# A hybrid encoder layer on one core: rounded bias product, joined value products, and the recurrent row factor behind the projection

## The chip, the core and the metric

The kernel runs on one core of a Trainium2 chip. A core has a matrix engine (TensorE, PE in the profile, with its weight loads as PEld), a vector engine (VectorE, DVE), an activation engine (ScalarE, ACT), GpSimd (POOL), a queue engine (SyncE, SP) and 16 DMA engines that all queues share. The metric is the device time of one execution in microseconds; for several runs the median is given.

## The reference, cut to what matters

One encoder layer for a sequence of 512 positions and a width of 1024, in float32:

```python
h = rms_norm(x, attn_norm_g)
xr, gate, q, k, v = split(h @ w_in)
xr = centred_depthwise_conv(xr, conv_w, conv_b)
y_rnn = (rg_lru(xr, fwd) + rg_lru(xr, bwd)) * gelu(gate)
y_attn = dilated_attention(q, k, v, rel_bias)      # 8 heads of 64, three dilated windows
mix = concat([rms_norm(y_rnn, norm_rnn_g), rms_norm(y_attn, norm_attn_g)])
x = x + mix @ w_out
x = x + square(relu(rms_norm(x, mlp_norm_g) @ w_up)) @ w_down
return rms_norm(x, final_norm_g)
```

The three windows of the attention are computed as one: a key counts as often as windows hold it, and the logarithm of that count, or -1e30 for a key in none, joins the relative bias in one table over the distance. That table is the "bias table" of this document. An RMSNorm divides each position by the root of its mean square; that factor is one number per position, a "row factor", and may be applied behind a matrix product that mixes features only.

## The kernel before, in words

Activations lie with features on the 128 partitions and the 512 positions along the free axis, so a projection of 128 output features is a chain of products of 128 x 128 by 128 x 512. Each float32 operand is split into a rounded high part (dtype fp32r) and a residue; `mm3` makes three rounded products of them (high x high, high x low, low x high). ScalarE makes the high parts (`conv_hi`, L192, tile whi) and VectorE the residues (`conv_lo`, L199, tile wlo) of every weight block. Blocks come through SyncE's queue into three buffers wraw; the next one is asked for when `conv_lo` has read the last. Products of plain float32 operands are used for transposes (`pt`, `prow`), for column sums (`pcs`), for the bias table and for the value products.

The order on every engine is written out by hand. The stages that matter here:

1. The input projection's first three blocks (pxr), the column sums of squares and the first row factor (`rstd_cols`, `row_tile`). The recurrent gate weights come on SyncE's queue (gwr, L231). On ScalarE's queue come relt (33 x 8: the bias of each of 32 buckets for 8 heads, and a row of ones) and oht (two halves of 33 x 512: one-hot rows for the distances, and the row with the logarithm).
2. A loop of 32 steps n for the value projection (pv). Between its steps stand the recurrent gates (`lru_gate`, pg, evacuated by ScalarE into ga), `lru_x` (VectorE, L407) and, at n == 18, `bias_prep`: two products of relt and oht (L348), negated by VectorE (nbs, L350), written to DRAM (nbd) and read back per head as overlapping rows (tw).
3. The gate projections, then q and k for pair 0 of heads.
4. A loop over five rounds i of four steps u. Step (i, u) makes the scores of pair i for query tile u (`att_s`, `att_e`), the transposes of pair i-1's exponentials (`att_t`) and some of its value products (`att_av`). Into this loop a list of fillers puts q and k of the next pairs and, behind them, `wo_thunks(0, c2)`: the output projection of the recurrent half. A dictionary `plan` keyed (i, u, slot) holds the rest: squares (`sq_`), their sum (`add`), column sums (`rnn_cols`), the row factor (`rnn_rows`), the multiplication by it (`scaled`), and the splits (`hi`, `lo`).
5. The output projection of the attention half, then the feed-forward block, which takes more than half of the time and is not touched.

Tiles of 128 x 512 share a pool of 48 buffers (tag "g"); the PSUM banks are four of tag "pj" (projections, value products, bias), two of "gs" and two of "et".

The value products of a pair are eight: four key tiles times two heads of 64 columns each, which write the two halves of one PSUM tile. They are issued in two calls:

```python
            if u == 2 and i >= 1:
                att_av(i - 1, (0, 1))
...
            if u == 0 and i >= 2:
                att_av(i - 2, (2, 3))
```

Of the kernel before, what the change touches and what calls it, by code (L numbers as in the profile page):

```python
# [12 lines left out]
FT = mybir.dt.float32  # L13
FR = mybir.dt.float32r
AF = mybir.ActivationFunctionType
OP = mybir.AluOpType

P = 128
S = 512
D = 1024  # L20
KD = D // P
NH = 8
DH = 64
NBUCK = 32
# [16 lines left out]
for _n, _w in (("ag", 8), ("w0", 4), ("w1", 4), ("w2", 4), ("w3", 4), ("cb", 4),  # L41
# [2 lines left out]
    VEC[_n] = _o  # L44
    _o += _w
NVEC = _o


def bias_onehot():
    rel = np.arange(-(S - 1), S)  # L50
    m = np.zeros(rel.shape, np.int64)
    for window, dil in PATTERNS:
        half = window // (2 * dil)
        m += (rel % dil == 0) & (np.abs(rel) <= half * dil)
    nb = NBUCK // 2
    me = nb // 2
    n = np.abs(rel)
    nf = np.maximum(n, 1).astype(np.float32)
    large = me + (np.log(nf / np.float32(me)) / np.float32(math.log(MAXD / me))
                  * np.float32(nb - me)).astype(np.int32)  # L60
    large = np.minimum(large, nb - 1)
    bucket = np.where(rel > 0, nb, 0) + np.where(n < me, n, large)
    oh = np.zeros((NBUCK + 1, 2 * S), np.float32)
    oh[NBUCK, :] = NEG
    idx = np.arange(rel.size)
    keep = m > 0
    oh[bucket[keep], idx[keep]] = 1.0
    oh[NBUCK, idx[keep]] = np.log(m[keep].astype(np.float64)).astype(np.float32)
    return oh


@with_exitstack
def hybrid_kernel(ctx: ExitStack, tc, xw, xT, w_in, w_v, w_out, w_up, w_dn, gates, vecs, rel, onehot, fg, out):
    nc = tc.nc
    consts = ctx.enter_context(tc.tile_pool(name="consts", bufs=1))
    big = ctx.enter_context(tc.tile_pool(name="big", bufs=1))
    stream = ctx.enter_context(tc.tile_pool(name="stream", bufs=3))
    work = ctx.enter_context(tc.tile_pool(name="work", bufs=1))
# [6 lines left out]
    NG = 48  # L85

    def g_(name, dt=FT, shape=(P, S)):
        return work.tile(list(shape), dt, name=name, tag="g", bufs=NG)
# [7 lines left out]
    def f(t):  # L96
        return t.bitcast(FT)
# [237 lines left out]
            mm3(pxr[t], wk(t, k), hk(k), False, k == KD - 1)  # L335


    relt = consts.tile([NBUCK + 1, NH], FT, name="relt")
    nc.scalar.dma_start(relt, rel)
    oht = [work.tile([NBUCK + 1, S], FT, name="oht", tag="g", bufs=NG) for _ in range(2)]  # L340
    for i in range(2):
        nc.scalar.dma_start(oht[i], onehot[:, i * S:(i + 1) * S])
    nbd = dram.tile([NH, 2 * S], FT, name="nbd")

    def bias_prep():
        for i in range(2):
            pbz = ps_("pbias", "pj")
            nc.tensor.matmul(pbz[0:NH, :], lhsT=relt, rhs=oht[i], start=True, stop=True)  # L348
            nbs = g_("nbs", shape=(NH, S))
            nc.vector.tensor_scalar(nbs, pbz[0:NH, :], -1.0, None, op0=OP.mult)  # L350
            nc.scalar.dma_start(nbd[:, i * S:(i + 1) * S], nbs)
# [135 lines left out]
    def y_hi(k, y):  # L487
        ycat[k] = (g_("yh", FR), g_("yl", FR))
        act(ycat[k][0], y, AF.Copy, scale=vec("yg", k))

    def y_lo(k, y):
        hi, lo = ycat[k]
        stt(lo, y, vec("yg", k), f(hi), op0=OP.mult, op1=OP.subtract)

    yrnn = {}
    rr = {}
# [6 lines left out]
    def rnn_rows():  # L503
        rr[0] = row_tile(rc[0], "et")

    def rnn_scaled(*ts):
        for t in ts:
            nc.vector.tensor_tensor(yrnn[t], yrnn[t], rr[0], op=OP.mult)

    def rnn_split(*ts):  # L510
        for t in ts:
            y_hi(t, yrnn[t])
        for t in ts:
            y_lo(t, yrnn.pop(t))

    def proj_thunks(c, tag, done):
        o = {}

# [58 lines left out]
    def lru_hooks(n):  # L577
        m = n - GA
        if m in (11, 12, 14, 15):
            lru_x({11: 0, 12: 1, 14: 2, 15: 3}[m])  # L580
        if m in (12, 13, 20, 22):
            lru_exp({12: 0, 13: 1, 20: 2, 22: 3}[m])
        if m in (16, 17, 27, 28):
            t = {16: 0, 17: 1, 27: 2, 28: 3}[m]
            lru_sqrt(t)
            scans.extend(scan_ops(t)[:4])
        if n in SC:
            scans.popleft()()
# [4 lines left out]
    for n, (k, tt) in enumerate(steps):  # L593
        c = C_V + k // 2
        if k == 0:
            pv[tt] = ps_("pv", vtag[tt])
        hi, lo = splits[c]
        sl = slice((k % 2) * S, (k % 2 + 1) * S)
        tsl = slice(tt * P, (tt + 1) * P)
        mm3(pv[tt], (h_hi[:, k, tsl], h_lo[:, k, tsl]), (hi[:, sl], lo[:, sl]), k == 0, k == KD - 1)  # L600
        if n >= 16:
            feed(c, n % 8)
        if n in (8, 11, 14):
            conv_hi({8: 6, 11: 7, 14: 8}[n])
        if n in (9, 12, 15):
            conv_lo({9: 6, 12: 7, 15: 8}[n])
        if n >= GA and n < GA + 12 and (n - GA) % 3:
            t, m = (n - GA) // 3, 2 * ((n - GA) % 3 - 1)
            lru_gate(t, m)
            lru_gate(t, m + 1)  # L610
        if n == 0:
            conv_lo(5)
            conv_b(2)
        if n == 2:
            conv_b(3)
        if n == GA + 1:
            conv_h(2)
            conv_c(2)
        if n == GA + 2:
            conv_h(3)  # L620
            conv_c(3)
        lru_hooks(n)
        if n == 18:
            bias_prep()
            load_tw(0)
            load_tw(1)
    vs = big.tile([P, 4, S], FT, name="vs", tag="bigC")
    last = [scan_ops_end(t) for t in range(4)]
# [115 lines left out]
    def att_av(p, jts):  # L744
        if 0 in jts:
            pav[p] = ps_("pav", "pj")
        for jt in jts:
            for e in range(2):
                a = slice(64 * e, 64 * e + 64)
                h = 2 * p + e  # L750
                nc.tensor.matmul(pav[p][a, :], lhsT=vs[:, jt, h * DH:(h + 1) * DH], rhs=et.pop((h, jt)),  # L751
                                 start=jt == 0, stop=jt == 3)
        if 3 in jts:
            y = g_("yp")
            nc.vector.tensor_tensor(y[:, ::-1], pav.pop(p), zrow.pop(p), op=OP.mult)
            y_sq(y, 1)
            y_hi(4 + p, y)
            y_rest[p] = y
# [16 lines left out]
    x1 = {}  # L775
# [6 lines left out]
    def wo_thunks(half, c2):  # L782
        c = C_WO + half * 4 + c2
        o = {}

        def mk(j, k):
            def run():
                if k == 0:
                    o["p"] = ps_("pwo", "pj")
                mm3(o["p"], wok(c, j, k), ycat[half * 4 + k], k == 0, k == 3)  # L790
                feed_q(c, 4 * j + k)
                if k == 3:
                    cc = 2 * c2 + j
                    nc.vector.tensor_tensor(x1[cc], x1[cc], o["p"], op=OP.add)
            return run
        return [mk(j, k) for j in range(2) for k in range(4)]

# [31 lines left out]
    def rnn_sq(t):  # L829
        y_sq(yrnn[t], 0)  # L830

    def scaled(t):
        return lambda: rnn_scaled(t)

    def hi(t):
        return lambda: y_hi(t, yrnn[t])

    def lo(t):
        return lambda: y_lo(t, yrnn.pop(t))

    def end(t):
        return lambda: rnn_end(t)

    def sq_(t):
        return lambda: rnn_sq(t)

    def add():
# [3 lines left out]
    plan = {(0, 0, 2): [sq_(0), add], (0, 0, 3): [end(1)],  # L851
            (0, 1, 1): [sq_(1)],
            (0, 2, 3): [add],
            (1, 0, 2): [end(2)], (1, 0, 4): [sq_(2)],
            (1, 1, 0): [add], (1, 1, 2): [end(3)], (1, 1, 4): [sq_(3)],
            (1, 2, 0): [add], (1, 2, 2): [rnn_cols], (1, 3, 1): [rnn_rows],
            (1, 3, 3): [scaled(0)], (1, 3, 4): [scaled(1), hi(0), hi(1)],
            (2, 1, 2): [lo(0), lo(1)], (2, 1, 3): [scaled(2), scaled(3), hi(2), hi(3)], (2, 2, 2): [lo(2), lo(3)]}
    for i in range(3):
        for key, (is_k, fn, e) in {(0, 2): (1, s_hi, 0), (0, 3): (1, s_hi, 1), (1, 0): (1, s_lo, 0), (1, 1): (1, s_lo, 1),  # L860
                                   (2, 2): (0, s_hi, 0), (2, 3): (0, s_hi, 1), (3, 0): (0, s_lo, 0), (3, 1): (0, s_lo, 1)}.items():
# [13 lines left out]
    for i in range(5):  # L875
        for u in range(4):
            if i < 4:
                att_s(i, u)
                if u == 0 and i < 3:
                    load_tw(2 * i + 2)  # L880
                if u == 2 and i < 3:
                    load_tw(2 * i + 3)
            if i >= 1:
                att_t(2 * i - 2, u)
                att_t(2 * i - 1, u)
            if i < 4:
                att_e(i, u)
            if u == 2 and i >= 1:
                att_av(i - 1, (0, 1))
            if u == 0 and i >= 1:  # L890
                att_z(i - 1)
            if u == 0 and i >= 2:
                att_av(i - 2, (2, 3))
            beside(i, u, 0)
            fill(1)
            beside(i, u, 1)
            fill(1)
            if u == 1 and i >= 1:
                att_r(i - 1)
            if u == 0 and i >= 2:  # L900
                att_y(i - 2)
            beside(i, u, 2)
            fill(1)
            beside(i, u, 3)
            fill(1)
            beside(i, u, 4)
# [25 lines left out]
    wo_b(0, 0)  # L932
    wo_b(0, 1)
    conv_hi(c + 3)
    att_av(3, (2, 3))
    att_y(3)
    wo_b(0, 2)
    for k in range(3):
# [160 lines left out]
    ts = None  # L1099
    nr2 = {}  # L1100
    for half in range(2):
# [4 lines left out]
        start = 0  # L1106
        if half == 0:
            start = 3
# [13 lines left out]
        for ff in range(start, HF):  # L1122
            p = ps_("pu", "pj")
# [12 lines left out]
            if ff == 11 - 8 * half:  # L1136
                if half == 0:
                    ts = big.tile([P, NQ, 1024], FT, name="ts", tag="bigA")
# [57 lines left out]
        for j in range(7 * NQ):  # L1196
            _, w, q = seq[j]
# [94 lines left out]
```

## Time and profile before

| | |
|---|---|
| median of 3 runs | 569.79 us (569.21 to 570.31) |
| profiled execution | 569.28 us |
| its span, first to last instruction | 567.5 us |
| TensorE busy | 555.4 us (98%) |
| VectorE busy | 388.8 us (69%) |
| ScalarE busy | 313.7 us (55%) |
| moved by DMA | 82.97 MB, 146 GB/s over the span |
| mean granted TensorE clock | 0.996 |

Times in rows of the profile are microseconds from the start of the span unless marked ns. A row of a timeline gives start, length, engine, line, operation, "out<-in", partitions x elements and count, and in brackets how long the engine was idle before it and what ended that. Matmuls are pipelined: one starts before the last has ended, so the distance of two starts tells what one costs. A float32 matmul appears as two records. In rows of waits the columns are the total, the number of waits and the longest.

### The profile page before, as it was taken

The numbers are of one execution on the slowest core, as the hardware profiler recorded it, in microseconds if no ns is written. First come the engines' busy times: TensorE is split into PE (matmuls) and PEld (weight loads), VectorE is DVE, ScalarE is ACT, GpSimd is POOL, SyncE is SP. The second block draws the span as 40 slices with busy tenths as digits, with TensorE's granted clock in tenths as the row PEclk, the third lists the DMA queues.
The fourth block names the chain that finished last, engine by engine and source line by source line (L and its number), as shares of the span: only waits on it lengthen the run. The fifth ranks groups of instructions, "written<-read, shape, count | busy, mean of one in ns | idle before, by whom it ended". The sixth has DMA issues, their size and how long they took to land.

```text
span 567.5 us, 6886 instructions
## 1 busy us (share of the span) xinstructions
PE 555.4 (98%) x2520; PEld 444.8 (78%) x2520; DVE 388.8 (69%) x610; ACT 313.7 (55%) x510; POOL 50.1 (9%) x70
## 2 busy tenths in 40 slices
PE   9999999999999999999999999999999999999993
PEld 7877788677777768888888888888888888888782
DVE  6696499986865429553468778978243676896894
ACT  7659993687865525245354466653223243665654
POOL 3450000000000000000002133001000000131000
PEclk9999999999999999999999999999999999999998
DMA  7623424453261112242239799959623234699603
GB/s 261 233 74 113 147 102 142 110 160 121 75 223 38 51 59 77 76 148 75 79 111 288 173 268 273 262 174 254 196 74 112 74 112 94 196 252 262 161 1 148
DMA packets 25494, 82.97 MB, mean 146 GB/s; under 512 B 3106, under 2 KB 3234, under 8 KB 25460
## 3 DMA queue, kind: packets, MB, share of 16 engines
q1 hardware_dynamic: 19968, 64.50, 33.1%
q0 software_dynamic: 4608, 16.78, 15.5%
q10 hardware_dynamic: 884, 1.25, 0.6%
q8 instruction: 20, 0.33, 0.2%
q14 instruction: 14, 0.11, 0.1%
HBM read 78.81 MB, written 2.13 MB: 143 GB/s over the span
## 4 chain that ended last, share of the span: by engine, by line
PE 80%; DVE 10%; DMA 4%; ACT 3%; issue 2%; SPq 0%; ACTq 0%; DVEq 0%
PE pu L223 10%; PE pu L224 10%; PE pu L225 10%; PE pd L224 6%; PE pd L223 6%; PE pd L225 6%; PE pqk L223 3%; PE pwo L223 3%; DVE wlo L199 3%; PE pav L751 3%; PE pqk L225 3%; PE pwo L225 3%; PE pwo L224 3%; PE pqk L224 3%; PE pt L718 2%; DMA wraw<-in_w_dn_dram 2%
## 5 line engine op out<-in xcount | busy, mean ns | idle before, releaser
L199 DVE TENSOR_TENSOR wlo<-wraw,whi 128x1024 fp32r<-128x1024 f32 x81 | 99.9, 1234 | 38.4 <-ACT whi L192 38.3
L192 ACT ACTIVATE whi<-wraw 128x1024 fp32r<-128x1024 f32 x81 | 85.5, 1055 | 40.0 <-PE pd L225 17.7
L223 PE MATMUL pu<-h2h,whi 128*128 128x512 f32 x256 | 100.4, 392 | 0.0
L225 PE MATMUL pu<-h2h,wlo 128*128 128x512 f32 x256 | 99.7, 390 | 0.0
L224 PE MATMUL pu<-h2l,whi 128*128 128x512 f32 x256 | 99.6, 389 | 0.0
L224 PE MATMUL pd<-wlo,ah 128*128 128x512 f32 x192 | 74.8, 390 | 0.4 <-DVE wlo L199 0.4
L223 PE MATMUL pd<-whi,ah 128*128 128x512 f32 x192 | 74.7, 389 | 0.0
L225 PE MATMUL pd<-whi,al 128*128 128x512 f32 x192 | 74.7, 389 | 0.0
L1015 ACT ACTIVATE a<-pu 128x512 f32<-128x512 f32 x32 | 19.0, 598 | 97.9 <-PE pu L225 97.9
L1016 DVE TENSOR_TENSOR a<-a 128x512 f32<-128x512 f32 x32 | 22.0, 691 | 65.8 <-ACT a L1015 65.8
L225 PEld LDWEIGHTS pu<-h2h,wlo 128*128 128x128 f32 x256 | 48.0, 188 | 10.1
L223 PEld LDWEIGHTS pu<-h2h,whi 128*128 128x128 f32 x256 | 48.1, 188 | 9.8
L224 PEld LDWEIGHTS pu<-h2l,whi 128*128 128x128 f32 x256 | 48.1, 188 | 9.7
L224 PEld LDWEIGHTS pd<-wlo,ah 128*128 128x128 f32 x192 | 36.0, 188 | 8.1 <-DVE wlo L199 0.8
L223 PEld LDWEIGHTS pd<-whi,ah 128*128 128x128 f32 x192 | 36.0, 188 | 7.5
L225 PEld LDWEIGHTS pd<-whi,al 128*128 128x128 f32 x192 | 36.0, 188 | 7.5
L192 ACT ACTIVATE whi<-ts 128x1024 fp32r<-128x1024 f32 x24 | 25.5, 1060 | 23.7 <-PE pd L225 17.7
L199 DVE TENSOR_TENSOR wlo<-ts,whi 128x1024 fp32r<-128x1024 f32 x24 | 29.3, 1221 | 8.4 <-ACT whi L192 8.0
L223 PE MATMUL pqk<-h_hi,whi 128*128 128x512 f32 x64 | 26.5, 414 | 0.0
L205 POOL DMA_DIRECT2D ts<-in_w_dn_dram x16 | 16.9, 1203 | 106.7 <-DVE wlo L199 106.7
L223 PE MATMUL pwo<-yh,whi 128*128 128x512 f32 x64 | 26.3, 412 | 0.0
L720 ACT ACTIVATE ett<-pt 128x512 f32<-128x512 f32 x32 | 17.3, 591 | 15.7 <-PE pt L718 15.7
(210 smaller groups left out, 1029.5 us busy)
## 6 DMA issues: line engine op xcount, KB each, us to landing
wraw<-in_w_up_dram SPq DMA_DIRECT2D x32, 512.0 KB, 3.3
wraw<-in_w_dn_dram SPq DMA_DIRECT2D x24, 512.0 KB, 6.7
ts<-in_w_dn_dram POOLq DMA_DIRECT2D x24, 512.0 KB, 12.1
wraw<-in_w_in_dram SPq DMA_DIRECT2D x13, 512.0 KB, 3.3
wraw<-in_w_out_dram SPq DMA_DIRECT2D x8, 512.0 KB, 3.3
ts<-in_w_dn_dram SPq DMA_DIRECT2D x8, 512.0 KB, 4.9
tw<-in_w_dn_dram SPq DMA_DIRECT2D x8, 512.0 KB, 6.2
tw<-in_w_dn_dram POOLq DMA_DIRECT2D x8, 512.0 KB, 11.4
```

The source lines that it names most:

```text
L192: act(hi, raws[i], AF.Copy)
L199: nc.vector.tensor_tensor(lo, r, f(splits[i][0]), op=OP.subtract)
L205: nc.gpsimd.dma_start(r, wblock(c[0], nxt[1], c[2]), accum_op=OP.add)
L223: nc.tensor.matmul(o, lhsT=a[0], rhs=b[0], start=bool(first), stop=False)
L224: nc.tensor.matmul(o, lhsT=a[0], rhs=b[1], start=False, stop=False)
L225: nc.tensor.matmul(o, lhsT=a[1], rhs=b[0], start=False, stop=bool(last))
L718: nc.tensor.transpose(pt[:, qt * P:(qt + 1) * P], en[h][qt][:, jt * P:(jt + 1) * P], ident)
L720: act(t, pt, AF.Copy)
L751: nc.tensor.matmul(pav[p][a, :], lhsT=vs[:, jt, h * DH:(h + 1) * DH], rhs=et.pop((h, jt)), start=jt == 0, stop=jt == 3)
L1015: act(r, p, AF.Relu)
L1016: nc.vector.tensor_tensor(r, r, r, op=OP.mult)
```

## The change

Three edits.

The first concerns the bias table. The three inputs of the table are laid out on 97 rows: the 32 buckets, the 32 buckets again, the last row, 31 rows of zeros, and the last row again; relt is also padded to 128 columns. `bias_round` makes rounded copies of both, in which the second copy of the bias holds the residue of the rounding, and the last row of oht holds the residue of the logarithm's row. One rounded product then sums high and low parts. `bias_round` runs on VectorE at steps n = 14 (relt and the first half) and n = 16 (the second half).

The second puts all eight value products of a pair into one call, where the second call stood.

The third no longer multiplies y_rnn by its row factor before the output projection. The splits are made from the unscaled values, and each of the eight output sums is multiplied by the row factor when it is read from PSUM, before it is added to x. The squares, column sums, row factor and splits stand at other places of the plan.

```diff
+NB3 = 3 * NBUCK + 1
...
+def bias_rows(a):
+    b, last = a[:NBUCK], a[NBUCK:]
+    return np.concatenate([b, b, last, np.zeros((NBUCK - 1, a.shape[1]), np.float32), last], axis=0)
...
-    relt = consts.tile([NBUCK + 1, NH], FT, name="relt")
+    relt = consts.tile([NB3, P], FT, name="relt")
     nc.scalar.dma_start(relt, rel)
-    oht = [work.tile([NBUCK + 1, S], FT, name="oht", tag="g", bufs=NG) for _ in range(2)]
+    oht = [work.tile([NB3, S], FT, name="oht", tag="g", bufs=NG) for _ in range(2)]
...
+    ohr = []
+    relr = consts.tile([NB3, P], FR, name="relr")
+
+    def bias_round(i):
+        if i == 0:
+            r = slice(NBUCK, 2 * NBUCK)
+            nc.vector.tensor_copy(relr, relt)
+            nc.vector.tensor_tensor(relr[r], relt[r], f(relr)[r], op=OP.subtract)
+        t = work.tile([NB3, S], FR, name="ohr", tag="g", bufs=NG)
+        ohr.append(t)
+        r = slice(3 * NBUCK, NB3)
+        nc.vector.tensor_copy(t, oht[i])
+        nc.vector.tensor_tensor(t[r], oht[i][r], f(t)[r], op=OP.subtract)
...
-            nc.tensor.matmul(pbz[0:NH, :], lhsT=relt, rhs=oht[i], start=True, stop=True)
+            nc.tensor.matmul(pbz, lhsT=relr, rhs=ohr[i], start=True, stop=True)
...
-    def rnn_scaled(*ts):
-        for t in ts:
-            nc.vector.tensor_tensor(yrnn[t], yrnn[t], rr[0], op=OP.mult)
...
         lru_hooks(n)
+        if n in (14, 16):
+            bias_round((n - 14) // 2)
         if n == 18:
             bias_prep()
...
-                    nc.vector.tensor_tensor(x1[cc], x1[cc], o["p"], op=OP.add)
+                    t = g_("wot")
+                    nc.vector.tensor_tensor(t, o["p"], rr[0], op=OP.mult)
+                    nc.vector.tensor_tensor(x1[cc], x1[cc], t, op=OP.add)
...
-            (1, 0, 2): [end(2)], (1, 0, 4): [sq_(2)],
-            (1, 1, 0): [add], (1, 1, 2): [end(3)], (1, 1, 4): [sq_(3)],
-            (1, 2, 0): [add], (1, 2, 2): [rnn_cols], (1, 3, 1): [rnn_rows],
-            (1, 3, 3): [scaled(0)], (1, 3, 4): [scaled(1), hi(0), hi(1)],
-            (2, 1, 2): [lo(0), lo(1)], (2, 1, 3): [scaled(2), scaled(3), hi(2), hi(3)], (2, 2, 2): [lo(2), lo(3)]}
+            (1, 0, 2): [end(2)],
+            (1, 1, 0): [sq_(2)], (1, 1, 2): [end(3)], (1, 1, 4): [add],
+            (1, 3, 0): [sq_(3)], (1, 3, 2): [hi(0)], (1, 3, 3): [add, hi(1)], (2, 0, 2): [rnn_cols],
+            (2, 0, 0): [lo(0), lo(1)], (2, 0, 4): [hi(2)],
+            (2, 1, 1): [rnn_rows], (2, 1, 2): [hi(3)], (2, 1, 4): [lo(2)], (2, 2, 3): [lo(3)]}
...
-            if u == 2 and i >= 1:
-                att_av(i - 1, (0, 1))
...
             if u == 0 and i >= 2:
-                att_av(i - 2, (2, 3))
+                att_av(i - 2, range(4))
...
-    att_av(3, (2, 3))
+    att_av(3, range(4))
```

In the order of instructions, TensorE has the same number of products; VectorE has six more for the tables, eight more behind the projection and four fewer before it. The loads of the tables keep their place in ScalarE's queue and carry 97 rows.

More of the change, by code (lines that the diff above doesn't have):

```diff
@@ L68, in bias_onehot @@
     oh[NBUCK, idx[keep]] = np.log(m[keep].astype(np.float64)).astype(np.float32)
-    return oh
+    return bias_rows(oh)
+def bias_rows(a):
+    b, last = a[:NBUCK], a[NBUCK:]
+    return np.concatenate([b, b, last, np.zeros((NBUCK - 1, a.shape[1]), np.float32), last], axis=0)
 @with_exitstack
@@ L504, in rnn_rows @@
         rr[0] = row_tile(rc[0], "et")
-    def rnn_scaled(*ts):
-        for t in ts:
-            nc.vector.tensor_tensor(yrnn[t], yrnn[t], rr[0], op=OP.mult)
[L510 to L514, printed above, removed]
     def proj_thunks(c, tag, done):
@@ L830, in rnn_sq @@
         y_sq(yrnn[t], 0)
-    def scaled(t):
-        return lambda: rnn_scaled(t)
     def hi(t):
@@ L1276 @@
     arrs["vecs"] = cont(np.concatenate([cols(v[n]) for n in VEC], axis=1))
-    arrs["rel"] = cont(np.concatenate([a["rel_bias"], np.ones((1, NH), np.float32)], axis=0))
+    arrs["rel"] = cont(np.pad(bias_rows(np.concatenate([a["rel_bias"], np.ones((1, NH), np.float32)], axis=0)), ((0, 0), (0, P - NH))))
     arrs["onehot"] = bias_onehot()
```

## The prediction

> **What bounds the kernel now.** I read the page first (engine totals, the chain, the DMA queues), then who waited for whom on TensorE, then the timeline around the three edits.
>
> ```profile
> span 567.5 us, 6886 instructions
> PE 555.4 (98%) x2520; PEld 444.8 (78%) x2520; DVE 388.8 (69%) x610; ACT 313.7 (55%) x510; POOL 50.1 (9%) x70
> PE 80%; DVE 10%; DMA 4%; ACT 3%; issue 2%; SPq 0%; ACTq 0%; DVEq 0%
> ```
>
> ```profile
> PE pg L223 <- ACT ga L401: 0.9, 2, 0.7
> PE pv L224 <- DVE wlo L199: 0.6, 1, 0.6
> ```
>
> TensorE is busy for 555.4 of 567.5 us. Between its first stage and its last it waits for other engines in three places only, all between 38 and 46 us: 0.9 us for ScalarE in two waits and 0.6 us for a weight residue. So a microsecond of TensorE work that goes is worth a microsecond at the end, and VectorE and ScalarE work costs nothing until one of TensorE's operands is late. Before 46 us the reverse holds: a chain through VectorE is behind those waits, and what delays it is paid in full.
>
> **Bias table.** The profile before shows both products of the table as one group between value-projection products.
>
> ```profile
> 55.47 0.39 PE L225 MATMUL pv<-whi,h_lo 128*128 128x512 f32 x1
> 55.79 1.88 PE L348 MATMUL pbias<-oht,relt 33*8 33x512 f32 x4
> 57.60 0.50 PE L223 MATMUL pv<-whi,h_hi 128*128 128x512 f32 x1
> ...
> 59.09 0.39 PE L223 MATMUL pv<-whi,h_hi 128*128 128x512 f32 x1
> ...
> 60.45 0.39 PE L223 MATMUL pv<-whi,h_hi 128*128 128x512 f32 x1
> ```
>
> Columns are start and length in us; matmuls overlap, so what counts is the distance between starts. From 59.09 to 60.45 lie six rounded products: 0.227 us each. The two float32 products are four records 0.43 us apart ((1.88 - 0.59 of the last) / 3), and entering and leaving them costs more: 55.47 to 57.60 is 2.13 us. From 55.47 to 59.09 there are 3.62 us for the two bias products and seven others. With the bias products rounded (fp32r) those are nine products of 0.227, 2.04 us. That removes 1.58 us. More rows in the contraction (97 for 33) and more output columns (128 for 8) cost nothing by these rows: the 128-row, 128-column products beside them are the ones that take 0.227.
>
> The rounding goes to VectorE: six instructions in two calls of bias_round, where there were none.
>
> ```profile
> 51.27 1.22 DVE L199 TENSOR_TENSOR wlo<-wraw,whi 128x1024 fp32r<-128x1024 f32 x1 [2.04 <-ACT whi L192]
> 52.41 3.69 DVE L407 TENSOR_TENSOR ga<-ga,xc 128x512 f32<-128x512 f32 x6
> 56.85 0.68 DVE L350 TENSOR_SCALAR nbs<-pbias 8x512 f32<-8x512 f32 x1 [0.74 <-PE pbias L348]
> ```
>
> ```profile
> L794 DVE TENSOR_TENSOR x<-x,pwo 128x512 f32<-128x512 f32 x8 | 5.5, 688 | 14.0 <-PE pwo L225 14.0
> L731 DVE COPY rzb<-rz 128x512 f32<-128x512 f32 x4 | 1.7, 427 | 0.1
> ```
>
> (The second fence groups the whole run: busy us, mean ns, idle us before.) The six are a copy and a subtraction on the narrow relt, and a copy and a one-row subtraction for each half of the table. A 512-wide copy takes 0.43 us; the 8-partition nbs takes 0.68, so a one-row subtraction is no cheaper than a full one and also takes 0.68. The first call stands ahead of the wlo of 51.27, which VectorE waited 2.04 us for: about 0.5 for the two on relt (estimate from the same widths) plus 0.43 plus 0.68 is 1.6 us, inside that gap. The second comes after four of the six ga products: (3.69 - 0.68)/5 is 0.60 each, so it begins at 52.41 + 2.41 = 54.82, the copy ends at 55.25 and the subtraction at 55.93 or a little later. TensorE would issue the second bias product at 55.47 + 2 x 0.227 = 55.93. The cover is exactly used up, and restarting costs something too (entry and exit of the float32 group together were 3.62 - 7 x 0.227 - 4 x 0.43 = 0.31). I take 0.15 us, bounds 0 and 0.4 (every dependent VectorE step fully serialised). Behind the second call stand two ga products and nbs; nbs is followed by the table's way through DRAM, which the scores use only in the head loop, so nobody else is late.
>
> **Value products.** The count stays at 32; four groups of four leave and four groups become eight.
>
> ```profile
> 142.33 1.04 PE L718 MATMUL pt<-ident,e 128*128 128x128 f32 x8
> 143.30 1.94 PE L751 MATMUL pav<-ett,vs 128*64 128x512 f32 x8
> 145.17 0.50 PE L223 MATMUL pqk<-h_hi,whi 128*128 128x512 f32 x1
> ...
> 146.66 0.39 PE L223 MATMUL pqk<-h_hi,whi 128*128 128x512 f32 x1
> ...
> 148.93 1.03 PE L718 MATMUL pt<-ident,e 128*128 128x128 f32 x8
> 149.72 0.48 PE L223 MATMUL pqk<-h_hi,whi 128*128 128x512 f32 x1
> ...
> 151.20 0.60 PE L302 MATMUL prow<-ident,rzb 128*128 128x128 f32 x4
> ```
>
> ```profile
> 143.78 1.03 PE L751 MATMUL pav<-ett,vs 128*64 128x512 f32 x4
> ```
>
> Eight transposes, a group of four value products and six rounded products take 146.66 - 142.33 = 4.33 us. The same without value products takes 151.20 - 148.93 = 2.27. So a separate group costs 2.06 us. Inside it the two heads run side by side: two pairs of records in 1.03 us, the last lasting 0.59, so a pair starts each 0.44 (0.43 by the bias records, which I use). Four more products in a group that is already open are four pairs, 1.72 us. Each join saves 0.34 us of entry and exit, four joins 1.36 us. The removed groups all stand behind transposes, as the measured one does. The data is ready: the products of the first two key tiles only move later, to where the other two already stood. What moves with them is the release of four ett buffers and the hold on one PSUM bank, shorter now.
>
> **Row factor.** Four multiplications by rr[0] leave VectorE, eight come (PSUM times row, then the addition that was there), at 0.69 like the addition L794 above: 2.7 us more VectorE work. The eight come where the additions stand, before which VectorE was idle 14.0 us in all, so the 5.5 us of the eight have cover. The squares and the splits yh and yl keep their number and only change place on ScalarE and VectorE. TensorE's pcs and prow come some steps later and cost the same there. New wait: the first wot waits for rr[0], and behind it on VectorE stand a weight residue and the score minima. prow goes out in step (2,1), the first output sum ends in step (2,3), and a step took 6.6 us (142.33 to 148.93), so the row is there. Cost 0; bounds 0 and 0.5 (one score row late by most of a multiplication).
>
> **The wider tables in the DMA queues.** This is the part that speaks against the change: relt grows from 33x8 to 97x128 (1 to 50 KB) and each oht from 33 to 97 rows (66 to 199 KB), issued on ScalarE's queue just when the recurrent gate weights come in.
>
> ```profile
> q10 hardware_dynamic: 132, 0.14, 2.4%
> oht<-in_onehot_dram ACTq DMA_DIRECT2D x2, 66.0 KB
> ```
>
> ```profile
> 17.53 5.51 DMA gwr<-in_gates_dram
> 23.06 0.63 ACT gwh L368
> 23.69 0.95 ACT whi L192
> 24.64 0.52 ACT gwh L368
> 25.16 0.49 ACT rrow L316
> 25.68 1.29 DVE xr L376 x2
> ...
> 36.34 2.23 DVE wlo L199
> ```
>
> ```profile
> 14.50:26.00 11.50, 11.50 (x58) 9.65 (x57) 7.23 (x13) 6.71 (x11) 4.01 (x3) 1.00 0.81 280
> 26.00:49.00 23.00, 21.50 (x93) 16.80 (x92) 19.95 (x24) 16.43 (x25) 10.40 (x16) 1.00 0.21 72
> ```
>
> The second fence is the chain of waits: the first gate load lands at 23.06, and from there ScalarE, then VectorE without a gap, lead to the wlo that TensorE waits for. A gate load that lands later delays TensorE by as much. The first fence (queues between 12 and 30 us) tells how the tables travel: 132 packets are 3 x 33 rows and 33 more, eleven to a transfer. I read these as one closing write for each engine used: 33 rows go on eleven engines, a divisor of 33. 97 has no divisor but one, so I expect each wide table on a single engine. The Trainium skill, "DMA: Bandwidth & Descriptors", section "Why a DMA increments its semaphore by 16 and not by 1", says just that: the largest number up to 16 that divides the rows, and a prime count of rows puts all on one. The 132 packets agree with it for 33 rows; no row here shows a prime count.
>
> The last two columns of the third fence are the busy share of the DMA engines and GB/s: a busy engine moves 280/16/0.81 = 21.6 GB/s. 50 KB is 2.3 us, 199 KB is 9.2 us, all three 20.7 us of one engine. That engine also carries a sixteenth of the rest: 280 x 11.5/16 = 201 KB up to 26 us (9.3 us) and 72 x 23/16 = 104 KB (4.8 us) up to 49. From 14.2 us the last table is in at 14.2 + 20.7 + 9.3 + 4.8 = 49.0 at the latest, and is used at 54.8; the first half is in 9 us sooner and used at 49.6. So the tables are in time. For the gates it matters what goes ahead of them on that engine. If rows take turns, relt's 512-byte rows (24 ns each at 21.6 GB/s) stand in front of the tables, and the engine's 8 rows each of the three weight loads ahead of the gates and of the first gate load let 32 of relt's pass: 0.8 us at most, less what the engine idled (0.19 of the time). Other engines gain a little, since they no longer carry table rows. I take 0.3 us, bounds -0.2 and 1.5; the rivals take the larger cases.
>
> **The sum.** -1.58 - 1.36 + 0.15 + 0.3 = -2.49 us. The profiled execution took 569.28 us (span 567.5); the median of the three runs is 569.79, 0.51 above it. 569.28 - 2.49 = 566.8 profiled, 569.79 - 2.49 = 567.3 by the runs.
>
> **Rivals.** A, slower: the engine with the tables serves transfers in long turns, not row by row, and the first gate share waits for relt and a whole table half, 11.5 us from 14.2, then for one weight load's share (33 KB, 1.5 us) and its own 16 KB: about 28 us in place of 23.06, 5 us late. Then -1.58 - 1.36 + 0.15 + 5 = +2.2, 572.0 us. It decides once the gates are more than 2.8 us late. For it: 16 engines are 0.81 busy there and the gate load alone bounds the chain. Against: 512-byte rows go first, and four gate loads follow each other so that only the first two count. 0.13.
>
> A2: the engine takes some 17 rows from one queue before it turns to the other. That makes four turns of relt, 17 x 24 ns = 0.4 us each, ahead of the first gate share: 1.6 us late, in sum -1.2, 568.6 us. The rows here give packets, not their order of service. 0.10. The Trainium skill, "DMA: Bandwidth & Descriptors", section "Queues, rings and completion order", has such turns: a whole packet, typically 9 to 17 descriptors, before an engine changes queues.
>
> B: the joins give nothing, because eight products in a row hold back the transposes or their buffers by as much as the switches cost. Then -1.58 + 0.45 = -1.1, 568.7 us. Against it: ScalarE and VectorE have gaps of 1 to 4 us in each step of the head loop. 0.07.
>
> C: the second table half lands late (a third less rate on the one engine: 20.7 becomes 31, so 59 instead of 49) and TensorE stands 4 us at the bias product: +1.5, 571.3 us. 0.03.
>
> **Numbers.** Forecast 0.67, A 0.13, A2 0.10, B 0.07, C 0.03. A measurement of this kernel tells about 0.2% (1.1 us) from no change. Faster by more is below 568.65: the forecast but for its upper end (0.64), half of A2 and about half of B, 0.72. The same: what is left of these three, 0.12. Slower: A and C, 0.16. The range leaves out A and C. Its upper end takes every upper bound at once, -1.58 - 1.36 + 0.4 + 0.5 + 1.5 = -0.54, 569.2, and holds A2 and B; its lower end takes the lower ones, -3.14, 566.65, and 0.3 for the spread of the runs (569.21 to 570.31): 566.3.
>
> **What would show it.** Right: pbias as two records of 0.39 us; four pav groups of 16 records about 3.7 us long and none of 8; gwh still starting near 23 us; TensorE's waits near 1.5 us in all plus at most 0.3 at pbias; 97-row loads leaving 98 packets each, so 294 in place of 132 in q10. Wrong: gwh at 25 us or later with a longer wait of pv for wlo (A, A2); a wait of pbias for VectorE over 0.5 us (C); new waits of pt, ps or pav in the head loop (B), or of wot for rrow.

## The result, and the profile after

The changed kernel takes 568.33 us (median of 22 runs, 567.19 to 569.41 but for one disturbed run), the kernel before 569.26 us (22 runs): a ratio of 0.9981, 95% interval 0.9975 to 0.9988, so 1.1 us faster (the medians by themselves differ by 0.9). Less than half of the forecast 2.5 us arrived. The profiled execution took 568.62 us.

The page of the kernel after (span; busy time by engine; shares of the chain that ended last):

```profile
span 566.8 us, 6889 instructions
PE 554.5 (98%) x2518; PEld 446.9 (79%) x2518; DVE 393.9 (69%) x620; ACT 313.3 (55%) x510; POOL 48.3 (9%) x70
PE 84%; DVE 6%; DMA 4%; ACT 3%; issue 1%; ACTq 1%; SPq 0%; DVEq 0%
```

TensorE is still the bound, and ScalarE's queue (ACTq), at 0% before, is on the chain. The places where the edits act, on TensorE's timeline:

```profile
57.84 0.39 PE L231 MATMUL pv<-whi,h_lo 128*128 128x512 f32 x1
58.06 0.90 PE L369 MATMUL pbias<-ohr,relr 97*128 97x512 f32 x2
58.80 0.40 PE L229 MATMUL pv<-whi,h_hi 128*128 128x512 f32 x1
...
140.02 1.04 PE L731 MATMUL pt<-ident,e 128*128 128x128 f32 x8
140.99 3.65 PE L764 MATMUL pav<-ett,vs 128*64 128x512 f32 x16
144.57 0.50 PE L229 MATMUL pqk<-h_hi,whi 128*128 128x512 f32 x1
```

The bias group is two records, and the distance from the product ahead of it to the one behind is 0.96 us (57.84 to 58.80) where it was 2.13. The value products of a pair are one group of 16 records. Both edits did on TensorE what they say. The starts of the same work in both profiles tell where the gain went:

| TensorE starts | before | after | shift |
|---|---|---|---|
| column sums of x | 20.59 | 21.14 | +0.56 |
| first pv | 29.48 | 34.05 | +4.57 |
| product ahead of the bias group | 55.47 | 57.84 | +2.37 |
| first gate projection | 66.57 | 67.66 | +1.09 |
| first score product | 103.38 | 104.47 | +1.09 |
| feed-forward block | 227.36 | 227.26 | -0.10 |

The bias group brings 1.27 us and the stretch of the scores 1.19 (behind the last row no edit acts, and the 0.6 us by which the spans differ further are not the change's), but at the bias group the kernel is 2.37 us late already. Of that, 0.55 is chance: the first load of x took 5.51 us in this profile and 4.96 in the one before (4.24 to 5.51 in those of the kernels below where it stands on the chain). The rest, 1.8 us, goes with the tables, as the waits below and the loads alone (under Experiments) show. The chain of waits of the kernel after (start, length, what), in order of time:

```profile
15.97 4.77 DMA wraw<-in_w_v_dram
20.74 0.02 issue
20.76 3.69 ACTq L348
24.45 0.05 issue
24.50 1.06 ACT whi L198
25.56 0.02 issue
25.59 1.24 DVE wlo L205
26.82 0.04 issue
26.86 0.50 PE pxr L231
27.37 0.60 PE prow L308 x4
27.97 0.43 PE pxr L229
28.40 0.42 PE pxr L230
```

L348 is the issue of a half of oht. The second one waits until 20.74 for a weight load, and then the instruction itself lasts 3.69 us; before, each lasted 0.30. The next on ScalarE is whi for the fourth block: its weights are there at 20.74, but it starts only when the issue has ended, at 24.50 in place of 19.77. TensorE's waits:

```profile
PE pxr L229 <- ACT whi L198: 1.3, 1, 1.3
PE pwarm L124 <- DVE epsb L115: 1.0, 1, 1.0
PE pxr L231 <- DVE wlo L205: 0.5, 1, 0.5
PE pxr L229 <- ACT w3h L264: 0.4, 1, 0.4
```

The first and third are new, 1.8 us. The waits of pg and pv of before, 1.5 us, are gone: TensorE comes later now than what they waited for. What the end of the chain shows is worse than the waits: after them a product takes 0.43 us, not 0.23. Two stretches of equal length (us, busy time of TensorE first; the last three columns are granted clock, DMA share and GB/s):

```profile
24.09:27.50 3.41, 1.58 (x7) 0.86 (x7) 1.23 (x1) 3.00 (x4) 1.35 (x1) 1.00 0.13 50
27.50:30.92 3.42, 3.42 (x11) 2.74 (x10) 2.28 (x3) 2.20 (x5) 3.16 (x6) 0.50 0.54 168
```

In 3.41 us TensorE was busy for 1.58, and for the next 3.41 us it was granted half its clock, which costs about 1.7 us (half of that stretch, an estimate). So 1.8 + 1.7 - 1.5, and the wait of 0.4 for w3h, which comes with the late x: 2.4 us, the shift at the bias group.

The tables themselves travelled as the prediction worked out. From 36 to 40 us they are alone in the queues:

```profile
36.00:40.00 4.00, 4.00 (x20) 3.30 (x19) 3.80 (x5) 3.08 (x5) 3.80 (x3) 1.00 0.06 25
```

And their queue between 5 and 60 us:

```profile
q10 hardware_dynamic: 294, 0.45, 2.3%
```

0.06 of 16 engines at 25 GB/s is one engine, and 294 packets are 3 x 98, one closing write to a table.

### The profile page after: what moved, and what is told of

Its sections match the earlier page's. It is cut to its first block, busy times and chain, and to the rows that moved or that the text cites. A ratio compares the mean times of both kernels' runs of the same rounds, so it can differ in the third digit from the quotient of the medians.

```text
span 566.8 us, 6889 instructions
## 1 busy us (share of the span) xinstructions
PE 554.5 (98%) x2518; PEld 446.9 (79%) x2518; DVE 393.9 (69%) x620; ACT 313.3 (55%) x510; POOL 48.3 (9%) x70
## 3 DMA queue, kind: packets, MB, share of 16 engines
q10 hardware_dynamic: 1046, 1.56, 0.8%
HBM read 79.12 MB, written 2.13 MB: 143 GB/s over the span
## 4 chain that ended last, share of the span: by engine, by line
PE 84%; DVE 6%; DMA 4%; ACT 3%; issue 1%; ACTq 1%; SPq 0%; DVEq 0%
PE pu L229 10%; PE pu L231 10%; PE pu L230 10%; PE pd L230 6%; PE pd L231 6%; PE pd L229 6%; PE pqk L229 3%; PE pwo L229 3%; PE pqk L231 3%; PE pwo L231 3%; PE pwo L230 3%; PE pqk L230 3%; PE pav L764 3%; PE pt L731 2%; DVE wlo L205 2%; DMA wraw<-in_w_dn_dram 2%
## 5 line engine op out<-in xcount | busy, mean ns | idle before, releaser
L718 ACT ACTIVATE e<-e,mn 128x512 f32<-128x512 f32 x32 | 22.8, 718 | 5.7 <-DVE mn L717 5.5
```

Of the source, the lines that this page charges most:

```text
L718: act(t, t, AF.Exp, scale=-1.0, bias=mn, accum_out=zs[p][:, 2 * qt + e:2 * qt + e + 1])
```

## Experiments

Ratios are to the kernel before, run beside each; 1% is 5.7 us. Differences in us are taken from the ratios; the medians alone can differ from them by 0.4 us.

**Rows that 16 engines share.**

```diff
-NB3 = 3 * NBUCK + 1
+NB3 = 112          # zeros below row 96
```

> The changed kernel with 15 more rows of zeros below the tables (112 rows, 16 times 7, in place of 97). The changed kernel's trace shows the second table half's issue holding ScalarE for 3.69 us, whi for the fourth block at 24.50 us in place of 19.77, TensorE waiting 1.8 us for it and then running 3.41 us at half clock. Theory H (97 rows go on one DMA engine, whose queue fills, and ScalarE is held at the issue): with 112 rows the issue takes about 0.3 us again, whi starts near 19.8 us, no half-clock stretch, and the time is 569.26 - 1.2 (bias) - 1.2 (joins) = 566.9 us. Rival V (the loss is in the volume of the tables, now larger still, or in the new VectorE steps): 568.3 us as with 97 rows, or a little more.

Measured 566.53 us, ratio 0.9954 (0.9942 to 0.9966): -2.6 us, as theory H said. ScalarE's timeline with 112 rows (both issues, the wait for a weight load between them included, take 2.82):

```profile
16.36 2.82 ACTq L349 DMA_DIRECT2D oht<-in_onehot_dram  x2
19.23 1.06 ACT L199 ACTIVATE whi<-wraw 128x1024 fp32r<-128x1024 f32 x1 [2.38 <-DMA wraw<-in_w_v_dram]
22.22 0.63 ACT L390 ACTIVATE gwh<-gwr 128x512 fp32r<-128x512 f32 x1 [1.94 <-DMA gwr<-in_gates_dram]
```

**The loads alone.** The kernel before, tables loaded with 97 rows, product as before.

```diff
-    relt = consts.tile([NBUCK + 1, NH], FT, name="relt")
+    relt = consts.tile([97, P], FT, name="relt")
...
-    oht = [work.tile([NBUCK + 1, S], ...
+    oht = [work.tile([97, S], ...
...
-            nc.tensor.matmul(pbz[0:NH, :], lhsT=relt, rhs=oht[i], ...
+            nc.tensor.matmul(pbz[0:NH, :], lhsT=relt[0:33, 0:NH], rhs=oht[i][0:33, :], ...
```

> The kernel before, whose three table loads are widened with zeros to 97 rows (and relt to 128 columns); the float32 product still reads the 33 rows, so nothing else differs. Theory H: only the loss of the front, about 1.4 us (1.8 us of waiting and 1.7 us of half clock, less the 1.5 us of later waits that it takes the place of, less what the clock's phase adds), so 570.7 us. Rival (the loss comes from the rounding steps on VectorE or from chance in the clock's start): 569.3 us, no change.

Measured 570.15 us, ratio 1.0024 (1.0015 to 1.0032): +1.4 us. The loss is reproduced without any of the new arithmetic:

```profile
18.64 4.43 ACTq L342 DMA_DIRECT2D oht<-in_onehot_dram  x2
23.12 1.06 ACT L192 ACTIVATE whi<-wraw 128x1024 fp32r<-128x1024 f32 x1 [5.42 <-issue]
24.08 0.61 ACT L368 ACTIVATE gwh<-gwr 128x512 fp32r<-128x512 f32 x1
```

In this profile the clock stayed at 1.00: whi came 1.4 us sooner than in the changed kernel and TensorE's waits for it and its residue were 0.3 and 0.5 us. The half clock is one way in which the loss is paid, not the only one.

**Another queue for the issue, the same engine for the rows.**

```diff
-        nc.scalar.dma_start(oht[i], onehot[:, i * S:(i + 1) * S])
+        nc.sync.dma_start(oht[i], onehot[:, i * S:(i + 1) * S])
```

> The changed kernel with 97 rows, but the two halves oht are issued on SyncE's queue, behind the gate loads; relt stays on ScalarE's. The halves still go on one DMA engine. Theory H (what costs is ScalarE held at the issue): SyncE is held for about 3.7 us instead, ScalarE starts whi at 20 us or a little later, and the time is about 567.2 us. Rival S (what costs is the one engine that all weight loads share with the tables, whoever issues them): gates and weights land as late as before, 568.3 us.

Measured 566.58 us, ratio 0.9953 (0.9941 to 0.9965): the whole loss is gone, with the tables still on one engine. ScalarE is free:

```profile
18.59 1.06 ACT L198 ACTIVATE whi<-wraw 128x1024 fp32r<-128x1024 f32 x1 [1.40 <-DMA wraw<-in_w_in_dram]
22.92 0.63 ACT L389 ACTIVATE gwh<-gwr 128x512 fp32r<-128x512 f32 x1 [3.27 <-DMA gwr<-in_gates_dram]
```

SyncE is held instead. Its issue of the second half lasts 3.19 us, to 23.48, and the weight load behind it is held longer still, 7.56 us from 23.58. The issues of the four loads of value weights (min/median/max ns), in the kernel before and in this one:

```profile
L186 SPq DMA_DIRECT2D wraw<-in_w_v_dram x4: 328/328/328, 15.4 to 28.2; - x4
L192 SPq DMA_DIRECT2D wraw<-in_w_v_dram x4: 328/435/7561, 15.0 to 31.3; - x4
```

Little depends on that load so early: TensorE's wait of pv for wlo is 0.8 us where it was 0.6. In the changed kernel, where ScalarE's queue carries the tables, SyncE's weight issue at 26.84 took 0.33 us although the engine was busy with table rows up to 43.5. In these kernels, then, the hold falls on the queue that carries the tables, on a second table half and on a weight load alike.

The gate weights are rounded at 22.92, waiting for their load alone. In both kernels with the halves on ScalarE's queue gwh followed whi without a wait for its load, and whi stood behind the issue; so what made ScalarE late was the held issue, and not the sharing of an engine (rival S). That the halves now also go behind the gates is a second difference, which on one engine was not tried apart.

**The joins alone.**

```diff
-            if u == 2 and i >= 1:
-                att_av(i - 1, (0, 1))
             if u == 0 and i >= 2:
-                att_av(i - 2, (2, 3))
+                att_av(i - 2, range(4))
...
-    att_av(3, (2, 3))
+    att_av(3, range(4))
```

> The kernel before with only the second edit: all eight value products of a head pair in one call. The prediction's term: four joins of 0.34 us, -1.36 us, so 567.9 us; the stretch from the q and k of pair 0 to the feed-forward block in the two traces says -1.2, so 568.1 us. Rival B (joins give nothing by themselves, the gain in that stretch is the row factor's): 569.3 us.

Measured 568.76 us, ratio 0.9997 (0.9988 to 1.0005): next to nothing, a miss. Its timeline of TensorE shows why:

```profile
132.32 0.39 PE L225 MATMUL pqk<-h_hi,wlo 128*128 128x512 f32 x1
133.43 1.02 PE L322 MATMUL pcs<-ones,ysq 128*128 128x1 f32 x8 [0.73 <-DVE ysq L483]
134.32 0.49 PE L223 MATMUL pqk<-h_hi,whi 128*128 128x512 f32 x1
```

The group that left this step no longer covers VectorE: the column sums of the recurrent half wait for the sum of squares. From the last product to pcs it is 1.11 us; six products and the sums' start take 2.35 us where they took 1.49 before, so 0.86 us are lost.

**The joins with the row factor's edit**, and **that edit alone**. The joins' diff is the one above; the edit's is that of the change, of which this decides:

```diff
-            (1, 2, 0): [add], (1, 2, 2): [rnn_cols], (1, 3, 1): [rnn_rows],
+            ... (2, 0, 2): [rnn_cols], ... (2, 1, 1): [rnn_rows],
```

> The kernel before with the second and the third edit (joined value products; row factor behind the projection, with its new places in the plan), tables as before. The joins alone gave a ratio of 0.9997: their trace shows the first joined step ending at the column sums of the recurrent half, which came 0.86 us late because VectorE's squares were not summed yet. Theory P (the joins are worth 1.2 us, and the third edit's plan, which puts these column sums two steps later, is what lets them be): 568.8 - 1.2 = 567.6 us, and no wait of pcs. Rival (the joins give nothing, the changed kernel's gain in that stretch has another source, the tables): 568.8 us.

Measured 567.83 us, ratio 0.9979 (0.9969 to 0.9989): -1.2 us, and no wait of pcs in the list of waits. Theory P holds.

> The kernel before with the third edit only (row factor behind the projection, new plan), value products still in two calls. The prediction's term: 0, so 568.8 us. Theory P says the same: by itself the plan moves work that nobody waits for. Rival R (the plan or the row factor is itself the source of the 1.2 us): 567.6 us.

Measured 569.27 us, ratio 1.0003 (0.9992 to 1.0014): nothing by itself. The third edit, whose plan puts rnn_cols at (2, 0, 2) in place of (1, 2, 2), lets the joins be worth their 1.2 us. The plan and the place of the multiplication were not run apart; that it is the plan follows from the wait of pcs, which comes with the joins alone and goes with the plan.

**The bias edit alone, on 112 rows**: the change's code for the table, in the kernel before, with the halves on ScalarE's queue and then on SyncE's.

```diff
+NB3 = 112
...
-            nc.tensor.matmul(pbz[0:NH, :], lhsT=relt, rhs=oht[i], start=True, stop=True)
+            nc.tensor.matmul(pbz, lhsT=relr, rhs=ohr[i], start=True, stop=True)
```

> The kernel before with the first edit only, on 112 rows (all 16 DMA engines). Prediction's terms: -1.58 + 0.15 = -1.43 us, 567.4 us; by the stretch around the bias products in the two traces -1.1 to -1.2, 567.6 us. Rival (the rounding steps on VectorE take back the gain elsewhere): 568.8 us.

Measured 568.54 us, ratio 0.9991 (0.9980 to 1.0001): -0.5 us, a miss by 0.7, though the bias group is as short as it should be. So the wider loads seemed to cost something on 16 engines too. Two kernels for that:

> The kernel before with the first edit alone on 112 rows, the halves issued on SyncE's queue behind the gate loads. On ScalarE's queue the same edit gave 0.9991 (-0.5 us, -1.1 to +0.1), where the stretch around the bias products is 1.2 us shorter. Theory W (the wider tables still cost something, 0.5 us or so, by their volume ahead of the gates): the full 1.2 us appear, 567.7 us. Rival (the start of those runs was late by chance, or the rounding on VectorE takes something): 568.4 us.

Measured 567.34 us, ratio 0.9971 (0.9962 to 0.9981): -1.65 us.

> The kernel before with table loads widened with zeros to 112 rows, the product still on the 33 rows: what the wider loads cost when they use all 16 DMA engines. Theory W (volume ahead of the gates): 0.5 us slower, 569.4 us. Rival (only the single engine cost anything): no change, 568.9 us.

Measured 569.69 us, ratio 1.0014 (1.0004 to 1.0024): +0.8 us. So the wider loads cost something in this kernel, as theory W said. Its mechanism, gates that land behind more bytes, is not shown. The kernel before_wide112 on ScalarE, where no issue is held (0.32 us each):

```profile
17.09 3.11 ACTq L342 DMA_DIRECT2D oht<-in_onehot_dram  x2
20.25 1.06 ACT L192 ACTIVATE whi<-wraw 128x1024 fp32r<-128x1024 f32 x1 [2.58 <-DMA oht<-in_onehot_dram]
24.03 0.63 ACT L368 ACTIVATE gwh<-gwr 128x512 fp32r<-128x512 f32 x1 [2.72 <-DMA gwr<-in_gates_dram]
```

gwh waits for its load until 24.03, where the kernel before has 23.06. But that load scatters as much when the tables have 33 rows. In the chains of waits it takes, in before_wide112 and then in before_joins, whose tables are those of the kernel before:

```profile
17.65 6.36 DMA gwr<-in_gates_dram
17.02 6.52 DMA gwr<-in_gates_dram
```

The kernel before has 5.51 there, and with the joins and the third edit gwh starts 4.68 us after the first gate load's issue (17.80 to 22.48). The price does not come out alike either. Moving the halves to SyncE's queue is worth 1.15 us in the bias edit alone (0.9991 to 0.9971), but 0.2 us in the changed kernel with 112 rows (0.9954 to 0.9951, at the end of this section), and there the rounding a step sooner is in it. With intervals of 0.5 to 0.9 us to either side of each, what the volume costs on 16 engines stays open.

The bias edit is worth 1.65 us once its tables travel behind the gates. It may be that a part of that is the 66 KB halves of before, which went ahead of them too; that was not tried.

**What holds the issue.** The kernel before with zeros to 83 and to 61 rows, both prime (relt too):

```diff
-    oht = [work.tile([NBUCK + 1, S], ...
+    oht = [work.tile([83, S], ...      # and 61
```

> The kernel before with table loads widened with zeros to 83 rows in place of 97 (83 is prime too: one DMA engine), the product still on the 33 rows. In both traces with 97 rows on ScalarE the second half's issue ended as the 7th row of the first half began: 2 x 98 less 6 descriptors, some 190, seem to be what can stand before one engine. Theory H with that depth: 2 x 84 = 168 fit, so the second issue takes about 0.25 us, and the time is 569.0 us, at most 0.4 above the kernel before. Rival S (one engine shared with the weights is what costs, in proportion to the rows): 86% of the 1.4 us, 570.0 us.

Measured 569.68 us, ratio 1.0004 (0.9993 to 1.0015). The time agrees with theory H, its number does not: the second issue lasted 2.58 us, not 0.25, and ended before the first row of the first half had begun.

```profile
18.95 3.65 ACTq L342 DMA_DIRECT2D oht<-in_onehot_dram  x2
22.64 1.06 ACT L192 ACTIVATE whi<-wraw 128x1024 fp32r<-128x1024 f32 x1 [4.89 <-issue]
```

By the time alone the depth of 190 would have passed for shown. That the time hardly moves looks like slack, by single profiles and so argued only: whi at 22.64 leaves TensorE one wait of 0.5 us for wlo; at 23.12 two of 0.8 in all; at 24.50 two of 1.8 and half a clock behind them. Against 19.77 the first three microseconds of delay cost little, the next two most of the loss.

> The kernel before with table loads widened with zeros to 61 rows (prime again: one DMA engine), the product still on the 33 rows. What ends the held issue of the second half is open: with 97 rows it ended as the 7th row of the first half began, with 83 rows before the first began (held for 2.58 us). Theory D (the line in front of one engine has a fixed depth, which the weights' descriptors share: 22 fewer descriptors could be let in 7 rows sooner): with 2 x 62 the second issue takes 0.3 us, ScalarE's whi starts near 20.5 us. Rival E (the issue waits for the engine to come to the first half at all, however many rows it has): held again for about 2.5 us.

Measured 569.06 us, ratio 1.0005 (0.9993 to 1.0016). The issues, one line of the trace (min/median/max ns):

```profile
L342 ACTq DMA_DIRECT2D oht<-in_onehot_dram x2: 232/234/237, 16.6 to 18.6; - x2
```

The second issue took 0.23 us and was over at 18.84, while the first half's first row began at 20.07. So the issue does not wait for the engine to come to the first half, whatever its rows (rival E falls). A line of fixed depth, counted in the tables' own rows, does not fit either: with 97 rows 189 of the two halves' 196 descriptors still stood in line when the issue ended, seven rows having begun, and with 83 rows 168 were not let in at once. 2 x 62 descriptors go in without a hold, 2 x 84 and 2 x 98 do not. What sets the limit, and whether the weights' descriptors count, these runs do not settle.

**A version that beats both.** 112 rows, the halves on SyncE's queue, and the second rounding a step sooner.

```diff
-        if n in (14, 16):
-            bias_round((n - 14) // 2)
+        if n in (14, 15):
+            bias_round(n - 14)
```

> The changed kernel with 112 rows, the halves oht issued on SyncE's queue behind the gate loads, and the rounding of the second half one step sooner (n = 15 in place of 16). Tables on all engines and behind the gates: if the tables' volume ahead of the gates costs anything, this is faster than 112 rows on ScalarE's queue (ratio 0.9954) by up to 0.6 us (two halves of 229 KB at about 300 GB/s, less what the 33 rows took), and the 0.25 us between the two bias products go: 568.9 - 2.6 - 0.25 = 566.0 us, and 565.4 with the volume. If neither matters, 566.3 us.

Measured 565.82 us, ratio 0.9951 (0.9937 to 0.9966): -2.8 us. It can't be told from 112 rows on ScalarE's queue (0.9954) by time, so the volume's cost does not show here; by the figures of the expectation itself (2 x 229 KB less 2 x 66 KB at 300 GB/s) it would be 1.1 us, not 0.6. The bias group lost its gap, 0.63 us for two records where the changed kernel has 0.90:

```profile
54.78 0.39 PE L232 MATMUL pv<-whi,h_lo 128*128 128x512 f32 x1
55.00 0.63 PE L370 MATMUL pbias<-ohr,relr 112*128 112x512 f32 x2
55.47 0.39 PE L230 MATMUL pv<-whi,h_hi 128*128 128x512 f32 x1
```

## Why the prediction was right, and where not

The direction was right (568.33 us lies in 566.3 to 569.2), the sum was not: -2.49 forecast, -1.1 measured. Step by step:

- **Bias products, -1.58.** Right. From the product ahead of the group to the first gate projection, 11.10 us became 9.54 in the version without the gap (54.78 to 64.32), 1.56 less. More rows and columns in the contraction cost nothing: the two products of 112 x 128 take 0.47 us there (55.00 to 55.47), and two products of 128 x 128 take 0.45.
- **The wait for the second rounding, +0.15 (0 to 0.4).** The changed kernel has 9.83 us there: the wait took 0.29. VectorE's timeline has the step as it was worked out, copy and one-row subtraction after four ga products, and the subtraction ends at 58.35, when the second product could go at 58.29; the rest is the restart.

```profile
54.79 2.49 DVE L428 TENSOR_TENSOR ga<-ga,xc 128x512 f32<-128x512 f32 x4
57.20 0.42 DVE L363 CAST ohr<-oht 97x512 fp32r<-97x512 f32 x1
57.66 0.69 DVE L364 TENSOR_TENSOR ohr<-oht,ohr 1x512 fp32r<-1x512 f32 x1
```

- **Joins, -1.36.** -1.19 in the profile and -1.2 in the runs, with the third edit. 0.34 a join was 0.30. What the step left out is that a join moves some 2 us of cover (2.06 for a separate group) away from one step and into another; alone, the joins ran into the column sums. Rival B had the size for that case and another cause.
- **Row factor, 0.** Right by itself (1.0003); with the joins its plan is what let them count.
- **Wider tables, +0.3 (-0.2 to 1.5).** This is the step that failed. The loads alone cost 1.4 us. The working followed bytes and rows through the engine and asked when the gates land; it never asked how long the issuing instruction itself takes when one engine has to take 196 descriptors, and so put that at nothing, though it named the queue, ScalarE's, on which whi and gwh stand behind it. The issue took 3.69 us in place of 0.30, and whi started at 24.50 in place of 19.77. Of the signs listed under "wrong" gwh came at 25.46, but not by rival A or A2: it started right behind whi without waiting for its load, and the longer waits were those of pxr for whi and wlo, while that of pv for wlo went. The upper bound of 1.5 held the size by luck, since it was made for another mechanism; so it is luck, too, that the measured 568.33 us lies near what A2 (568.6) and B (568.7) would give.

-1.27 - 1.19 + 1.4 = -1.06, close to the measured -1.1. The two gains are of single profiles and the 1.4 has an interval of 0.9 to 1.8, so the agreement is closer than the figures warrant.

Two rules were weighed. The Trainium skill, "DMA: Bandwidth & Descriptors", section "Why a DMA increments its semaphore by 16 and not by 1", puts a prime number of rows on one engine. The trace agrees for 97: one closing write to a table, and 25 GB/s at a share of 0.06. The Trainium skill, "DMA: Bandwidth & Descriptors", section "Queues, rings and completion order", has an engine drain a packet of typically 9 to 17 descriptors before it turns to another queue. The trace disagrees here: while weights were in the queues, rows of the first half began at 24.27, 24.43, 24.59 and 24.75, each taking 0.08 us, so one row of the table and one of the others took turns. Rival A2 had its turns from that rule.

## What to carry to other kernels

Count the engines a load will use and the descriptors each gets, and cost the issue as an instruction of the engine that issues it: a small table with an unlucky number of rows can hold up an engine that has work ready. Pad rows to a number that 16 divides, and issue what is needed late on a queue with nothing urgent behind it, since the loads behind it can be held too. When work is taken out of one step of an overlapped loop, look for what it covered, since a true gain can show as none until the next wait is moved too.

## What the hardware showed that was not expected

- Before 45 us the issue of a load lasted 0.23 to 0.86 us in all these profiles, on one engine too, but for those held: 2.6 to 3.7 us when one half of 83 or 97 rows stood in front of another, and 7.56 us for the weight load behind two halves of 97. The engine that issued it did nothing else meanwhile, ScalarE or SyncE alike.
- TensorE's clock was halved after a stretch of 3.41 us in which it had been busy for 1.58 us, its longest rest 1.3 us, and stayed so for 3.41 us. The Trainium skill, "TensorE: Matmul & The Clock Gate", section "Part 1: The HAM clock gate", gives the window as 3,413 ns and has the clock fall after one or more idle windows. The length agrees with the trace; here, though, TensorE was not idle in the window but busy for somewhat less than half of it.
- The first load of x took 4.24 to 5.51 us from one profile to the next with the same instructions ahead of it, so that single profiles differ by up to 1.3 us before the first product that matters; shifts under that are to be read against the runs.
